# A two-layer decoder trunk with routed experts: the rows of expert 0 gathered apart from those of its group

## The chip, the core and the metric

The kernel runs on one core of a Trainium2 chip. The metric is device time in microseconds (us) of one execution, as the median of several runs. A core has a tensor engine (PE; its weight loads are listed as PEld), a vector engine (DVE), a scalar engine (ACT), GpSimd (POOL), a sync engine (SP) whose queue issues nearly all transfers here, and 16 DMA engines that bring data from DRAM into SBUF. Matmul results land in PSUM, in eight banks of 512 float32 per partition.

## The reference, cut to what matters

Two layers, each a token mixer (forgetting attention, then retention) and a mixture of 32 SwiGLU experts in 4 groups. 256 tokens of width 1024. A router picks one group per token and two experts in it.

```python
D_MODEL = 1024; SEQ = 256; DEPTH = 2
N_GROUPS = 4; EXPERTS_PER_GROUP = 8; N_EXPERTS = 32; TOP_K = 2; EXPERT_FF = 512

def hier_moe(h, wr_g, br_g, wr_e, br_e, w_gu, w_down):
    p_group = jax.nn.softmax((xf @ wr_g).astype(F32) + br_g.astype(F32), axis=-1)
    pg, gi = lax.top_k(p_group, 1)
    ...
    pv, pi = lax.top_k(jax.nn.softmax(e_in, axis=-1), TOP_K)
    gates = pg * pv / jnp.sum(pv, axis=-1, keepdims=True)
    expert_id = gi * EXPERTS_PER_GROUP + pi
    return grouped_experts(xf, expert_id, gates, w_gu, w_down).reshape(B, S, D)

# grouped_experts: for every expert e, on the rows xb of its tokens
    a, b = jnp.split(xb @ w_gu[e], 2, axis=-1)
    return (jax.nn.silu(a) * b) @ w_down[e]

def reference(...):
    h = x
    for i in range(DEPTH):
        hn = rms_norm(h, norm_mix[i])
        if i % N_MIXERS == 0:
            h = h + forgetting_attention(hn, fox_w_in[j], fox_b_f[j], fox_w_out[j])
        else:
            h = h + retention(hn, ret_w_in[j], ret_gn_gain[j], ret_w_out[j])
        hn = rms_norm(h, norm_ffn[i])
        h = h + hier_moe(hn, ...)
    return rms_norm(h, norm_final)
```

The expert weights are most of the bytes: a gate and up matrix of 4 MB and a down matrix of 2 MB for each of 32 experts in each of two layers.

## The kernel before

**Weights.** SBUF holds 26 slots of 1 MB. One list names every weight in the order of use (attention, experts of layer 0, retention, experts of layer 1). `Stream.pump` walks that list on SP's queue: it issues the next transfer as soon as enough slots are free, beyond a number held back (`st.reserve`). `st.done(key)` gives a slot back after the last matmul that reads it, and the transfer that takes the slot waits on SP for that matmul. Of experts 0 to 9 and of 31 (`pieces(e) == 2`) the gate and up matrix comes as four transfers of 1 MB and the down matrix as two; the others come in transfers of 2 MB. Order on every engine is the order of the program text (`manual_schedule`).

**The router.** `phase_moe` begins when the residual rows `h` of the layer are complete. DVE works out the mask `mkf` of chosen experts; three small matmuls with triangular and all-ones matrices count ranks; `rk` (line 950) then holds, per token and expert, the token's place among that expert's rows (0 if it is not chosen). Each expert has up to `CAP` = 32 rows.

**The gather of a group of four experts.** `one_hots(g4)` (lines 954 and 956) builds `oh`, for two halves of 128 tokens and four experts a matrix of 32 columns each: 1 where the place is right, times the token's `rstd` (the norm's factor). `gather(xg, tag, tag_T)` then takes the rows of all four experts at once, as 128 rows by 1024, in two steps: `rows(n)` multiplies `oh` with half of the width of `h` (line 967, a float32 matmul of 512 columns is two instructions) and ACT copies the result to SBUF (line 968); `turn(n)` transposes four chunks of 128 columns on PE (line 974), and DVE multiplies them by the norm's gain on the way out of PSUM (line 975). The result `xg` holds eight chunks `kk` of 128 by 128, with 32 columns for each of the four experts.

**An expert.** `first_product` computes the gate and up product in eight chunks `kk` (line 1044, 64 instructions), giving back a slot after every second chunk for experts in 1 MB pieces; ACT takes the silu (line 1053), DVE multiplies (line 1054) and transposes (line 1061). The second product (line 1072, 32 instructions) uses the down matrix. Eviction is split between DVE and ACT (lines 1087, 1085). After four experts `scatter` adds the group's results into PSUM sums.

**Around expert 0.** `start(part)`, called in the first product of expert 0, places the gate values' DVE chain (`gates`, lines 991 to 1008) behind chunk 1, sets `st.reserve = 1` behind chunk 5, and claims a slot for scratch behind chunk 7; another scratch slot is claimed behind the second product. So the first, second and third of the four slots that expert 0's first product gives back are filled with new weights at once, and the next transfer takes a slot of expert 0's down matrix. The gather of the next group stands behind the third expert of each group; only that of experts 0 to 3 stands ahead of the first product of its group.

Of the kernel before, what the change touches and what calls it, by code (L numbers as in the profile page):

```python
# [17 lines left out]
ALU = mybir.AluOpType  # L18
# [3 lines left out]
P = 128  # L22
# [6 lines left out]
CAP = 32  # L29
# [198 lines left out]
def trunk(ctx, tc, x, fox_w_in, fox_b_f, fox_w_out, ret_w_in, ret_gn_gain, ret_w_out,  # L228
# [3 lines left out]
    mm = nc.tensor.matmul  # L232
    V, A, G, PE = nc.vector, nc.scalar, nc.gpsimd, nc.tensor
# [5 lines left out]
    def bank(tag, dtype=F32):  # L239
        bufs = {"acc": 4, "sc": 2, "pt": 1, "o": 1}[tag]  # L240
        return ps.tile([P, 512], dtype, name=tag, tag=tag, bufs=bufs)
# [123 lines left out]
    iota = cst[:, C_IOTA:C_IOTA + CAP]  # L365
# [551 lines left out]
    def phase_moe(l, g, reserve_after, ahead, before_last, between):  # L917
# [31 lines left out]
        keep_warm(3)  # L949
        V.scalar_tensor_tensor(rk, b[:, 0:64].rearrange("p (t e) -> p t e", t=2), 1.0, mkf, ALU.add, ALU.mult)  # L950

        def one_hots(g4):

            V.tensor_tensor(oh, rk[:, :, 4 * g4:4 * g4 + 4, None].to_broadcast([P, 2, 4, CAP]),
                            iota[:, None, None, :].to_broadcast([P, 2, 4, CAP]), ALU.is_equal)
            V.tensor_tensor(oh, oh, rstd[:, :, None, None].to_broadcast([P, 2, 4, CAP]), ALU.mult)  # L956

        def gather(xg, tag, tag_T):

            o = oh.rearrange("p t e s -> p t (e s)")  # L960
            halves = [xg[:, 4 * n:4 * n + 4, :] for n in range(2)]
            flat = [v.rearrange("p c q -> p (c q)") for v in halves]

            def rows(n):
                b = bank(tag)
                for t in range(2):
                    mm(b, o[:, t, :], h[:, t, 512 * n:512 * n + 512], start=t == 0, stop=t == 1)  # L967
                A.activation(flat[n], b, AF.Copy)

            def turn(n):  # L970
                b = bank(tag_T)
                hv = flat[n].rearrange("p (q c) -> p c q", c=4)
                for c in range(4):
                    PE.transpose(b[:, P * c:P * c + P], hv[:, c, :], ident)  # L974
                V.tensor_tensor(halves[n], b.rearrange("p (c q) -> p c q", c=4),  # L975
                                gT[:, gi, 4 * n:4 * n + 4, None].to_broadcast([P, 4, P]), ALU.mult)

            rows(0)
            rows(1)
            turn(0)  # L980
            turn(1)

        one_hots(0)
        gather(g.xg, "acc", "acc")


        mm(b[:, 64:96], onb, mkf[:, 0, :], start=False, stop=False, skip_group_check=True)
# [46 lines left out]
        def first_product(e, e4, xg, after_part):  # L1034
            bgu = bank("sc")
            for part in range(4):
                n = 2 // pieces(e)
                key = "gu", l, e, part // n
                w = st.get(key)[:, 2 * (part % n):2 * (part % n) + 2, :]
                for k in range(2):  # L1040
                    kk = 2 * part + k
                    wv = w[:, k, :].rearrange("p (two f) -> p two f", two=2)
                    for j in range(4):
                        mm(bgu[32 * j:32 * j + 32, 0:256].rearrange("p (two f) -> p two f", two=2),  # L1044
                           xg[:, kk, 32 * e4:32 * e4 + 32], wv[:, :, P * j:P * j + P],
                           start=kk == 0, stop=kk == 7, skip_group_check=True)
                if part % n == n - 1:
                    st.done(key)
                if WARM <= e < NE - 1:
                    keep_warm(2, "pt")  # L1050
                after_part(part)
            sl, gg, gTt = w2["sl"], w2["gg"], w2["gT"]
            A.activation(sl, bgu[:, 0:P], AF.Silu)  # L1053
            V.tensor_tensor(gg.rearrange("p (c q) -> p q c", c=4), sl.rearrange("p (q c) -> p q c", c=4),  # L1054
                            bgu[:, P:2 * P].rearrange("p (q c) -> p q c", c=4), ALU.mult)
            return gg, gTt

        def turned(gg, gTt):


            V.transpose(gTt, gg)

        def expert(e, e4, xg, y4, after_part):
            gg, gTt = first_product(e, e4, xg, after_part)
            turned(gg, gTt)
            by = bank("o")
            n = 4 // pieces(e)
            for j in range(4):
                key = "wd", l, e, j // n
                w = st.get(key)  # L1070
                for nb in range(4):
                    mm(by[32 * nb:32 * nb + 32, 0:256], gTt[:, 32 * j:32 * j + 32],  # L1072
                       w[:, j % n, 256 * nb:256 * nb + 256], start=j == 0, stop=j == 3, skip_group_check=True)
                if j % n == n - 1:
                    st.done(key)
                if j == 1 and e >= WARM:
                    keep_warm(2, "sc")
            if e == 0:
                third()
                y4 = w2["y4"][0]  # L1080
            for nb in range(4):
                o = y4[32 * e4:32 * e4 + 32, 256 * nb:256 * nb + 256]
                i = by[32 * nb:32 * nb + 32, 0:256]
                if nb % 2:
                    A.activation(o, i, AF.Copy)  # L1085
                else:
                    V.tensor_copy(o, i)  # L1087
# [490 lines left out]
```

## Time and profile before

| | |
|---|---|
| Median of 3 runs | 1248.16 us (1246.19 to 1248.6) |
| Profiled execution | 1251.0 us, of which span 1248.9 us |
| PE busy | 982.5 us (79%) |
| DVE busy | 414.3 us (33%) |
| ACT busy | 317.6 us (25%) |
| DMA | 462.20 MB, 90.8% of 16 engines' span on SP's queue |
| Line 967 (rows of a group) | 72.8 us in 112 instructions to one kind of bank, and 16 more to another |
| Line 1044 (gate and up product) | 277.4 us in 4096 instructions |

The span is the time from the first to the last instruction of the profiled execution; the execution's own time is 2.1 us longer. Layer 0's router starts at about 163 us of the span and layer 1's at about 803 us. Busy shares are averages over stretches with different limits, so the stretches around the two routers have to be read by themselves. In a row of the timeline the first number is the start and the second the length of a run of equal instructions (xN says how many); in brackets stands the idle time before it and what ended it.

### The profile page before, as it was taken

What the parts mean: (1) busy time and instruction counts of PE and PEld (TensorE: products, weight loads), DVE (VectorE), ACT (ScalarE), POOL (GpSimd) and SP (SyncE); (2) the same over time, 40 slices, a digit from 0 to 9 for tenths busy, and PEclk for the clock granted to TensorE, in tenths of its full rate; (3) what the DMA queues carried; (4) which work ended last, traced back from release to release, by engine and by line L of the source; (5) the groups of instructions that cost most, each with busy time, mean ns of one, the idle gap of its engine ahead of it and who ended that gap; (6) DMA issues with size and microseconds to landing.
All of it is one profiled execution on the core that took longest, in us unless ns stands there. A gap on an engine that the chain in (4) does not pass through costs nothing.

```text
span 1248.9 us, 21544 instructions
## 1 busy us (share of the span) xinstructions
PE 982.5 (79%) x9223; PEld 634.3 (51%) x9223; DVE 414.3 (33%) x927; ACT 317.6 (25%) x672; POOL 42.8 (3%) x49
## 2 busy tenths in 40 slices
PE   8999986777575756678999999977776767677777
PEld 8888863343232323334889888744332323233333
DVE  5676832121111111111677676422121111111112
ACT  5665621111010100100554575321110111010112
POOL 2000000000000000000133100000000000000000
PEclk9999999899887879898999999989999888888979
DMA  9975879999999999999992768889999999999995
GB/s 339 321 264 192 321 279 421 419 427 426 427 426 427 428 428 426 427 426 394 378 335 69 268 237 308 332 357 419 423 427 428 427 427 427 427 427 427 428 424 192
DMA packets 74406, 462.20 MB, mean 370 GB/s; under 512 B 8881, under 2 KB 13761, under 8 KB 42050
## 3 DMA queue, kind: packets, MB, share of 16 engines
q1 hardware_dynamic: 73600, 460.17, 90.8%
q8 instruction: 74, 1.21, 0.4%
q10 hardware_dynamic: 706, 0.60, 0.2%
q14 instruction: 26, 0.21, 0.0%
HBM read 459.70 MB, written 1.05 MB: 369 GB/s over the span
## 4 chain that ended last, share of the span: by engine, by line
DMA 49%; PE 29%; DVE 2%; issue 1%; ACT 1%; POOLq 0%; ACTq 0%; SPq 0%; DVEq 0%
DMA slot<-in_expert_w_gu_dram 29%; DMA slot<-in_expert_w_down_dram 19%; PE sc L1044 5%; PE acc L495 4%; PE acc L509 3%; PE acc L507 3%; PE acc L508 3%; PE o L1072 3%; PE sc L967 1%; PE acc L1098 1%; DMA slot<-in_ret_w_in_dram 1%; DVE slot L1087 1%; PE pt L528 0%; PE acc L1138 0%; ACT slot L1085 0%
## 5 line engine op out<-in xcount | busy, mean ns | idle before, releaser
L1044 PE MATMUL sc<-slot,slot 128*32 128x256 f32 x4096 | 277.4, 422 | 54.9 <-DMA slot<-in_expert_w_gu_dram 51.8
L1044 PEld LDWEIGHTS sc<-slot,slot 128*32 128x32 f32 x4096 | 138.5, 119 | 181.4 <-issue 69.6
L1072 PE MATMUL o<-slot,slot 128*32 128x256 f32 x1984 | 137.8, 422 | 101.4 <-DMA slot<-in_expert_w_down_dram 58.7
L1072 PEld LDWEIGHTS o<-slot,slot 128*32 128x32 f32 x1984 | 70.8, 119 | 164.8 <-issue 80.2
L1054 DVE TENSOR_TENSOR slot<-slot,sc 128x128 f32<-128x128 f32 x64 | 23.7, 371 | 388.2 <-ACT slot L1053 388.2
L462 DVE SCALAR_TENSOR_TENSOR slot<-slot,gT,slot 128x512 fp32r<-128x512 f32 x160 | 123.9, 794 | 52.3 <-ACT slot L451 50.9
L495 PE MATMUL acc<-slot,slot 128*128 128x256 f32 x960 | 125.8, 288 | 1.6 <-ACT slot L451 1.1
L451 ACT ACTIVATE slot<-slot,gT 128x512 fp32r<-128x512 f32 x160 | 111.4, 718 | 38.6 <-PE acc L495 15.4
L495 PEld LDWEIGHTS acc<-slot,slot 128*128 128x128 f32 x960 | 118.9, 193 | 4.2 <-ACT slot L451 1.7
L1087 DVE COPY slot<-o 32x256 f32<-32x256 f32 x124 | 51.8, 418 | 204.3 <-PE o L1072 177.1
L1085 ACT ACTIVATE slot<-o 32x256 f32<-32x256 f32 x124 | 46.5, 375 | 281.5 <-DVE slot L1087 281.5
L1053 ACT ACTIVATE slot<-sc 128x128 f32<-128x128 f32 x64 | 17.7, 277 | 374.4 <-PE sc L1044 374.4
L507 PE MATMUL acc<-slot,slot 128*128 128x512 f32 x256 | 102.5, 400 | 0.0
L508 PE MATMUL acc<-slot,slot 128*128 128x512 f32 x256 | 100.0, 391 | 2.1 <-DVE slot L462 2.1
L509 PE MATMUL acc<-slot,slot 128*128 128x512 f32 x256 | 100.1, 391 | 0.0
L967 PE MATMUL sc<-h,slot 128*128 128x512 f32 x112 | 72.8, 811 | 33.5 <-DVE slot L956 33.5
L1098 PE MATMUL acc<-slot,slot 128*128 128x512 f32 (+1 forms) x128 | 60.9, 611 | 13.4 <-ACT slot L1085 13.2
L967 PEld LDWEIGHTS sc<-h,slot 128*128 128x128 f32 x112 | 27.7, 258 | 74.6 <-issue 74.6
L508 PEld LDWEIGHTS acc<-slot,slot 128*128 128x128 f32 x256 | 48.2, 188 | 11.8 <-DVE slot L462 2.8
L509 PEld LDWEIGHTS acc<-slot,slot 128*128 128x128 f32 x256 | 48.0, 188 | 10.2
L507 PEld LDWEIGHTS acc<-slot,slot 128*128 128x128 f32 x256 | 48.2, 188 | 9.3 <-issue 0.3
L975 DVE TENSOR_TENSOR slot<-pt,gT 128x512 f32<-128x512 f32 x28 | 19.4, 691 | 96.5 <-PE pt L974 96.5
(237 smaller groups left out, 750.6 us busy)
## 6 DMA issues: line engine op xcount, KB each, us to landing
slot<-in_expert_w_gu_dram SPq DMA_DIRECT2D x84, 2048.0 KB, 39.1
slot<-in_expert_w_gu_dram SPq DMA_DIRECT2D x86, 1024.0 KB, 13.4
slot<-in_expert_w_down_dram SPq DMA_DIRECT2D x42, 2048.0 KB, 39.1
slot<-in_expert_w_down_dram SPq DMA_DIRECT2D x40, 1024.0 KB, 13.3
slot<-in_ret_w_in_dram SPq DMA_DIRECT2D x24, 1024.0 KB, 14.1
slot<-in_fox_w_in_dram SPq DMA_DIRECT2D x15, 1024.0 KB, 11.8
slot<-in_ret_w_out_dram SPq DMA_DIRECT2D x8, 1024.0 KB, 7.3
slot<-in_fox_w_out_dram SPq DMA_DIRECT2D x4, 1024.0 KB, 14.6
```

The source lines that it names most:

```text
L451: A.activation(wh, w, AF.Copy, scale=1.0 if g is None else g)
L462: V.scalar_tensor_tensor(wl, w, g, wh, ALU.mult, ALU.subtract)
L495: mm(o, w[:, P * j:P * j + P], x[:, k, :], start=first and k == 0 and j % 2 == 0, stop=last and k == 7, skip_group_check=True)
L507: mm(banks[t], xh[:, q], wh, start=first and k == ks[0], stop=False)
L508: mm(banks[t], xh[:, q], wl, start=False, stop=False)
L509: mm(banks[t], xl[:, q], wh, start=False, stop=last and k == ks[-1])
L967: mm(b, o[:, t, :], h[:, t, 512 * n:512 * n + 512], start=t == 0, stop=t == 1)
L1044: mm(bgu[32 * j:32 * j + 32, 0:256].rearrange("p (two f) -> p two f", two=2), xg[:, kk, 32 * e4:32 * e4 + 32], wv[:, :, P * j:P * j + P], ...
L1072: mm(by[32 * nb:32 * nb + 32, 0:256], gTt[:, 32 * j:32 * j + 32], w[:, j % n, 256 * nb:256 * nb + 256], start=j == 0, stop=j == 3, skip_gr ...
L1085: A.activation(o, i, AF.Copy)
L1087: V.tensor_copy(o, i)
L1098: mm(sums[t, n], w2["scm"][0:rows, P * t:P * t + P], y4[0:rows, 512 * n:512 * n + 512], start=start, stop=False, skip_group_check=True)
```

## The change

Expert 0 of each layer no longer takes its columns from the group's `xg`. Two DVE instructions build its one-hot columns alone (rank compare and factor in one step); 16 matmuls, two halves of tokens for each of eight chunks, take 128 columns of `h` (every fourth one) as the stationary operand and the 32 one-hot columns as the moving one, so that the result `x0` comes out as chunks that need no transposing. All eight chunks lie in one PSUM bank; DVE evicts four at a time with the gain. `one_hots(0, 1)` then builds the columns of experts 1 to 3, and the gather of the whole group stands between the first and the second product of expert 0. `x0` lies in the first two of the eight chunks of `g.xg`, which that gather later overwrites. The same code runs in both layers.

```diff
--- before.py
+++ after.py
@@ -949,11 +949,13 @@
         keep_warm(3)
         V.scalar_tensor_tensor(rk, b[:, 0:64].rearrange("p (t e) -> p t e", t=2), 1.0, mkf, ALU.add, ALU.mult)
 
-        def one_hots(g4):
-
-            V.tensor_tensor(oh, rk[:, :, 4 * g4:4 * g4 + 4, None].to_broadcast([P, 2, 4, CAP]),
-                            iota[:, None, None, :].to_broadcast([P, 2, 4, CAP]), ALU.is_equal)
-            V.tensor_tensor(oh, oh, rstd[:, :, None, None].to_broadcast([P, 2, 4, CAP]), ALU.mult)
+        def one_hots(g4, i=0):
+
+            n = 4 - i
+            V.tensor_tensor(oh[:, :, i:4, :], rk[:, :, 4 * g4 + i:4 * g4 + 4, None].to_broadcast([P, 2, n, CAP]),
+                            iota[:, None, None, :].to_broadcast([P, 2, n, CAP]), ALU.is_equal)
+            V.tensor_tensor(oh[:, :, i:4, :], oh[:, :, i:4, :],
+                            rstd[:, :, None, None].to_broadcast([P, 2, n, CAP]), ALU.mult)
 
         def gather(xg, tag, tag_T):
 
@@ -980,8 +982,20 @@
             turn(0)
             turn(1)
 
-        one_hots(0)
-        gather(g.xg, "acc", "acc")
+
+        x0 = g.xg[:, 0:2, :].rearrange("p a (k s) -> p (a k) s", s=CAP)
+        for t in range(2):
+            V.tensor_scalar(oh[:, t, 0, :], iota, rk[:, t, 0:1], rstd[:, t:t + 1], ALU.is_equal, ALU.mult)
+        bx = bank("acc")[:, 0:8 * CAP].rearrange("p (k s) -> p k s", k=8)
+        for n in range(2):
+            for c in range(4):
+                for t in range(2):
+                    hv = h[:, t, 512 * n:512 * n + 512].rearrange("p (q c) -> p c q", c=4)
+                    mm(bx[:, 4 * n + c, :], hv[:, c, :], oh[:, t, 0, :], start=n == 0 and c == 0 and t == 0,
+                       stop=t == 1, skip_group_check=True)
+            V.tensor_tensor(x0[:, 4 * n:4 * n + 4, :], bx[:, 4 * n:4 * n + 4, :],
+                            gT[:, gi, 4 * n:4 * n + 4, None].to_broadcast([P, 4, CAP]), ALU.mult)
+        one_hots(0, 1)
 
 
         mm(b[:, 64:96], onb, mkf[:, 0, :], start=False, stop=False, skip_group_check=True)
@@ -1061,8 +1075,10 @@
             V.transpose(gTt, gg)
 
         def expert(e, e4, xg, y4, after_part):
-            gg, gTt = first_product(e, e4, xg, after_part)
+            gg, gTt = first_product(e, e4, xg if e else x0, after_part)
             turned(gg, gTt)
+            if e == 0:
+                gather(xg, "acc", "acc")
             by = bank("o")
             n = 4 // pieces(e)
             for j in range(4):
```

On PE, at the start of the experts of layer 0, before (the names: `acc`, `sc` and `o` are PSUM banks, `slot_124` the slot with the router's data, `oh` and `xg`; a bracket names the engines or transfers that the first instruction waits for):

```order
L528 MATMUL o<-ones 128x128 x2
L967 MATMUL acc<-h,slot_124 128x512 [waits DVE_49]
L967 MATMUL acc<-h,slot_124 128x512 x3
L974 MATMUL acc<-ident,slot_124 128x128 [waits Activation_49]
L974 MATMUL acc<-ident,slot_124 128x128 x3
L974 MATMUL acc<-ident,slot_124 128x128 [waits Activation_49]
L974 MATMUL acc<-ident,slot_124 128x128 x3
L987 LDWEIGHTS onb
L987 MATMUL sc<-mkf,onb 128x32
L988 LDWEIGHTS onb
L988 MATMUL sc<-mkf,onb 128x32
L1044 MATMUL sc<-slot_135,slot_124 32x256 [waits DMAHW5_49,DMAHW1_49,DVE_49]
```

and now:

```order
L528 MATMUL o<-ones 128x128 x2
L994 MATMUL acc<-slot_124,h 128x32 [waits DVE_49] x2
L994 MATMUL acc<-slot_124,h 128x32 x6
L994 MATMUL acc<-slot_124,h 128x32 [waits DVE_49]
L994 MATMUL acc<-slot_124,h 128x32 x7
L1001 LDWEIGHTS onb
L1001 MATMUL sc<-mkf,onb 128x32
L1002 LDWEIGHTS onb
L1002 MATMUL sc<-mkf,onb 128x32
L1058 MATMUL sc<-slot_135,slot_124 32x256 [waits DMAHW5_49,DMAHW1_49]
```

Four wide matmuls and eight transposes ahead of the first product became sixteen narrow matmuls, with a wait for DVE in their middle, at the ninth; the first product itself (line 1044, now 1058) has lost its own wait for DVE.

On PE, from the end of expert 0's first product to the first chunk of expert 1, before:

```order
L1044 MATMUL sc<-slot_989,slot_124 32x256 x7
L1072 MATMUL o<-slot_991,slot_989 32x256 [waits DMAHW5_49,DVE_49,PE_49]
L1072 MATMUL o<-slot_991,slot_989 32x256 x7
L1072 MATMUL o<-slot_141,slot_989 32x256 [waits DMAHW6_49,DMAHW0_49]
L1072 MATMUL o<-slot_141,slot_989 32x256 x7
L1044 MATMUL sc<-slot_143,slot_124 32x256 [waits DMAHW7_49]
```

and now:

```order
L1058 MATMUL sc<-slot_989,slot_124 32x256 x7
L969 MATMUL acc<-h,slot_124 128x512 [waits DVE_49]
L969 MATMUL acc<-h,slot_124 128x512 x3
L976 MATMUL acc<-ident,slot_124 128x128 [waits Activation_49]
L976 MATMUL acc<-ident,slot_124 128x128 x3
L976 MATMUL acc<-ident,slot_124 128x128 [waits Activation_49]
L976 MATMUL acc<-ident,slot_124 128x128 x3
L1088 MATMUL o<-slot_991,slot_989 32x256 [waits DMAHW5_49,DVE_49]
L1088 MATMUL o<-slot_991,slot_989 32x256 x7
L1088 MATMUL o<-slot_141,slot_989 32x256 [waits DMAHW6_49,DMAHW0_49]
L1088 MATMUL o<-slot_141,slot_989 32x256 x7
L1058 MATMUL sc<-slot_143,slot_124 32x256 [waits DMAHW7_49,DVE_49]
```

The group's gather (now lines 969 and 976) moved in whole to the place between the two products of expert 0. SP's queue issues the same transfers in the same order as before.

## Rows read from the trace of the kernel before

**Rows 1.** Page, part 4: the chain that ended last, by engine.
```profile
DMA 49%; PE 29%; DVE 2%; issue 1%; ACT 1%; POOLq 0%; ACTq 0%; SPq 0%; DVEq 0%
```
**Rows 2.** Stretches: PE, PEld, DVE, ACT, POOL busy, then PE clock, DMA share, GB/s.
```profile
170.00:175.00 5.00, 4.72 (x43) 2.78 (x46) 1.66 (x5) 2.72 (x4) 0.00 (x0) 1.00 0.00 0
...
810.00:815.00 5.00, 4.72 (x50) 2.88 (x52) 2.03 (x8) 3.17 (x5) 0.00 (x0) 1.00 0.02 3
...
740.00:750.00 10.00, 10.00 (x49) 8.17 (x48) 7.74 (x13) 7.06 (x12) 0.00 (x0) 1.00 0.46 156
...
280.00:560.00 280.00, 187.20 (x2030) 92.32 (x2029) 41.73 (x100) 27.40 (x72) 0.00 (x0) 0.87 1.01 427
860.00:1200.00 340.00, 235.88 (x2616) 116.50 (x2612) 53.89 (x130) 35.15 (x93) 0.00 (x0) 0.88 1.01 426
```
**Rows 3.** Timeline of PE and DVE around the first expert of layer 0.
```profile
167.24 0.23 DVE L950 SCALAR_TENSOR_TENSOR slot<-sc,mkf 128x64 f32<-128x64 f32 x1 [0.46 <-PE sc L948]
167.50 0.43 DVE L954 TENSOR_TENSOR slot<-slot,cst 128x256 f32<-128x256 f32 x1
167.96 0.42 DVE L956 TENSOR_TENSOR slot<-slot,rstd 128x256 f32<-128x256 f32 x1
168.44 3.70 PE L967 MATMUL acc<-h,slot 128*128 128x512 f32 x8 [0.60 <-DVE slot L956]
...
171.98 0.63 PE L974 MATMUL acc<-ident,slot 128*128 128x128 f32 x4
...
172.72 0.69 DVE L975 TENSOR_TENSOR slot<-acc,gT 128x512 f32<-128x512 f32 x1 [4.33 <-PE acc L974]
...
172.89 0.75 PE L974 MATMUL acc<-ident,slot 128*128 128x128 f32 x4 [0.28 <-ACT slot L968]
...
173.61 3.66 PE L1044 MATMUL sc<-slot,slot 128*32 128x256 f32 x64
...
178.47 1.93 PE L1072 MATMUL o<-slot,slot 128*32 128x256 f32 x32 [1.20 <-issue]
...
180.19 3.66 PE L1044 MATMUL sc<-slot,slot 128*32 128x256 f32 x64
```
**Rows 4.** Timeline: instructions of nearly the new ones' shapes.
```profile
162.18 1.96 PE L565 MATMUL pt<-wr,slot 128*128 128x36 f32 x16
...
164.73 0.39 DVE L932 SCALAR_TENSOR_TENSOR slot<-pt,rstd,rb 128x32 f32<-128x32 f32 x2
...
177.65 0.37 DVE L1054 TENSOR_TENSOR slot<-slot,sc 128x128 f32<-128x128 f32 x1 [0.50 <-ACT slot L1053]
```
**Rows 5.** SP's timeline in three short windows: issues at the restart of layer 0.
```profile
174.74 0.33 SPq L166 DMA_DIRECT2D slot<-in_expert_w_gu_dram  x1
...
176.47 0.69 SPq L166 DMA_DIRECT2D slot<-in_expert_w_gu_dram  x1
...
179.59 0.33 SPq L166 DMA_DIRECT2D slot<-in_expert_w_down_dram  x1
```
**Rows 6.** DMA issues, us to landing: those three, one at 800.48, one at 815.98.
```profile
slot<-in_expert_w_gu_dram SPq DMA_DIRECT2D x1, 1024.0 KB, 5.4
...
slot<-in_expert_w_gu_dram SPq DMA_DIRECT2D x1, 1024.0 KB, 8.9
...
slot<-in_expert_w_down_dram SPq DMA_DIRECT2D x1, 1024.0 KB, 8.3
...
slot<-in_expert_w_down_dram SPq DMA_DIRECT2D x1, 1024.0 KB, 5.6
...
slot<-in_expert_w_gu_dram SPq DMA_DIRECT2D x1, 1024.0 KB, 10.8
```
**Rows 7.** Page, part 6: the same kind over the whole span, median to landing.
```profile
slot<-in_expert_w_gu_dram SPq DMA_DIRECT2D x86, 1024.0 KB, 13.4
```
**Rows 8.** Layer 1, expert 2: timeline row, and the stretch around it.
```profile
828.76 5.35 PE L1044 MATMUL sc<-slot,slot 128*32 128x256 f32 x64
...
829.50:832.80 3.30, 3.30 (x36) 1.65 (x32) 0.00 (x0) 0.00 (x0) 0.00 (x0) 0.50 1.01 427
```

## The prediction

> **What bounds the kernel now.** I read the page's chain first: almost half of it is transfers, a third PE [rows 1]. The stretches then say where each holds. In the long middle of either layer's experts the 16 DMA engines are busy without a break (share 1.01 at 427 GB/s over 280 us, 426 over 340 us), while PE works two thirds of the time [rows 2]. There the end is set by the bytes, and only time in which the DMA engines stand still can be won. In the retention mixer between the two layers PE is busy 10.00 of 10 us [rows 2], so whatever layer 0 gains or loses arrives at layer 1's router undiminished.
>
> The DMA engines do stand still around each router: the stretch from 170 to 175 us moved 0 GB/s, that from 810 to 815 us moved 3 [rows 2]. All slots are full by then, and the next transfer has to wait until expert 0's first product gives back a slot. The SP rows show it: issue at 174.74 us, 1.13 us behind the start of that product at 173.61 [rows 3, 5]. So the path that counts is: ranks ready, gather, first two chunks of expert 0's product, issue. It occurs twice, once per layer, and layer 1's rows repeat layer 0's. A microsecond off it is a microsecond off the end, if the DMA engines, once started, don't run dry again.
>
> **The change part by part, for layer 0.** `rk` is ready at 167.24 + 0.23 = 167.47 us [rows 3].
>
> One-hots. Before, two DVE instructions on 256 columns end at 168.38, and PE starts 0.06 later [rows 3]. Now two on 32 columns. This kind with two pointer operands on 32 columns isn't in the rows; the nearest pair took 0.39 for both [rows 4], and I take that: the first ends at about 167.7, the second at 167.9. The bounds are half of it and the old 0.88. PE, which waits for the first alone and is just done with its keep-warm matmuls, starts at about 167.8.
>
> Sixteen float32 matmuls are 32 instructions, each with its own 128-column weight load. Sixteen of the same kind with 36 columns took 1.96 us [rows 4], 0.12 each; they load adjacent columns, here it is every fourth. Four transposes with such a load took 0.63 [rows 3], 0.16 each with the drain of the last one in it. So a half takes 1.96 to 2.5; I take 2.1, near the row of the same length. The first half ends at 169.9.
>
> Now the wait. The ninth matmul waits for DVE, and the order leaves only one candidate, the first eviction: the first product, which reads that eviction's result, no longer waits for DVE itself. The eviction starts some 0.1 later (172.61 to 172.72 before [rows 3]) and takes between 0.30 (an estimate: 0.69 for 512 columns less 384 at 1.02 ns, the slope between 0.43 for 256 and 0.69 [rows 3]) and 0.37 [rows 4]: I take 0.33, to 170.3, and PE goes on at 170.4. The second half ends at 172.5. The first product started 0.03 before the last transpose ended, with the same two rank matmuls between (172.89 + 0.75 = 173.64, against 173.61 [rows 3]). It now starts at 172.5 instead of 173.6: **1.1 us earlier**. The second eviction has 1.8 us (half of the product) to finish in and hides there, as do `one_hots(0, 1)` and the gates' chain on DVE, which only has to end before the gather on PE does. Bounds for this part: 0.7 (slow one-hots, slow eviction) to 1.7 (no wait).
>
> The wait falls under a rule. In the old gather each eviction had a bank of its own, so PE went from one half to the next with no wait for DVE (its two waits are for the one-hots and for ACT's copy [rows 3]), and the trace can't show the price. The Trainium skill, page "PSUM — Partial Sum Buffer", section "PSUM bank collisions raise a hardware error", says that a bank is to be guarded as a whole on a 32-partition quadrant, not by address, since matmul writes and vector reads there must not coincide. Two halves in one bank are thus serialised although they share no column. By that rule the gain is the 1.1 above, by addresses alone it would be 1.7.
>
> The gather that moves. Between the products PE so far idled 1.20 us waiting for silu, product and transpose [rows 3]. Now it runs the gather there: from 168.44 to the rank matmul at 173.48 it occupied 5.04 us of PE's order [rows 3]. It starts 3.5 us into the first product (3.66 less the 0.2 by which expert 1's product started ahead of the end of the second product: 178.47 + 1.93 against 180.19 [rows 3]), that is at 176.0, and the second product starts at 181.06, not 178.47: **2.6 us later**, expert 1 with it. Behind this wait stand, on PE, the second product and all of the experts; on SP, the transfers that take the slots they give back. ACT's two copies and DVE's two evictions for the gather come after silu and the transpose, and delay nothing.
>
> What is late next. The three issues of expert 0's first product come 1.1 earlier, at 173.65 to 175.4. The fourth takes a slot of expert 0's down matrix and follows the second product by 179.59 - 178.47 = 1.12 [rows 3, 5]: now at 182.2. The third landed at 176.47 + 8.9 = 185.4 [rows 5, 6], now at 184.3 if the data follow as before. The fourth, which found the engines busy, landed 2.5 later, at 179.59 + 8.3 = 187.9 [rows 5, 6]; now that would be 186.8. But it is issued only 2.1 us ahead of the third's landing, and a transfer issued to idle or nearly idle engines took 5.4 and 5.6 us [rows 6], which makes 187.6 to 187.8. So of the 1.1 us between 0.1 and 1.1 survive. I take **0.45** in layer 0, near the rows of 5.4, since the ramp of a fourth transfer overlaps the third's end. From the fifth on (expert 1's first at 182.8 + 1.13 = 183.9, then one per 0.87 us, half of 174.74 to 176.47 [rows 5]) the queue fills faster than one per 2.5 us drains it.
>
> Another price for a transfer from rest: the Trainium skill, page "DMA: Bandwidth & Descriptors", section "Anatomy of one DMA — SWDGE (gpsimd) path", gives about 2.0 us plus bytes at 436 GB/s for another path of issue, an estimated 4.4 us for 1 MB. The trace's 5.4 and 5.6 decide. With 4.4 the fourth would land at 186.6, never late, and the sum would be the full 2.2.
>
> In layer 1 the third transfer took 10.8 to land, not 8.9 [rows 6], so a late fourth has more time; I take 0.8 there, between the same bounds. PE's 2.6 us of lateness at expert 1 cost nothing later on: such a transfer takes 13.4 us from issue to landing over the span [rows 7], against some 5.5 from rest, so about 8 us of queue cover it.
>
> The sum: 0.45 + 0.8, about 1.2 us less. The profiled execution took 1251.0 us (span 1248.9 and 2.1 around it), so 1249.8 there. It lies 2.8 above the median of 1248.16; the terms are absolute, so the median becomes **1247.0 us**. A measurement of this kernel can tell about 0.2% from no change, 2.5 us: the forecast lies below that.
>
> **The rivals.** *No wait between the halves, and no dry queue.* Both layers gain 1.7: 3.3 less, 1244.9. For it: the columns are disjoint. Against: the order shows the wait. Chance 0.12.
>
> *The transfers run dry and restart from rest.* The fourth lands at 187.8 or later, where it landed before: nothing is won in either layer, 1248.2. For it: 5.6 us; against: the third is still in flight. Chance 0.17.
>
> *The clock falls between the two products: slower.* PE's granted clock is 1.00 (2.4 GHz) in the stretches around both routers; it was 0.50 (1.2 GHz) in the stretch from 829.5 us, early in layer 1's experts, and a first product took 5.35 us there instead of 3.66 [rows 2, 3, 8]. The new narrow matmuls and the stop between the halves are thin work for PE. If the clock falls there, first product or gather loses 1.7 us, the fourth transfer is issued at 183.9 and lands at 189.3, 1.4 later than before. It decides from an issue later than 182.5. In both layers that makes 2.8 more, 1251.0; against it stands that 36-column matmuls of the same step run just ahead of both routers and the clock held. Chance 0.08.
>
> *The gather of expert 0 is no shorter than the old one.* Had its instructions the 0.16 of the transposes [rows 3] in full, the 32 would take some 0.9 us more, and with an eviction of the old 0.69 the gain is gone. The product starts when it did, and the fourth transfer lands about 1.0 later: 1250.1. Chance 0.05.
>
> **How the numbers follow.** The forecast has the remaining 0.58, with 1246.0 to 1248.0 as its own range. Faster by over 0.2% (below 1245.7) takes the first rival, some of the forecast's edge and of the runs' own scatter of 2.4 us: 0.17. Slower by over 0.2% (above 1250.7) takes most of the clock rival and a little scatter: 0.08. The rest is 0.75. The range, 1244.8 to 1249.8, takes in the first rival, the dry queue and part of the slower ones.
>
> **What would show it.** Right: the first of the narrow matmuls some 0.6 us earlier than the old gather began; PE idle about 0.7 us on DVE at the ninth matmul; the first product 1.1 us earlier and the second 2.6 later behind `rk`; a fourth issue 8.5 us behind the first one instead of 4.9; a zero-traffic stretch shorter by 1.1 us, and a dip of the DMA share some 9 us behind the restart. Wrong: no idle time at the ninth matmul; a step other than 0.12; a second stretch of zero traffic of over 1 us; a granted clock below 1.00 between `rk` and expert 1; or PE waits for weights before about 280 us that were not there before.

## The result: slower, and the profile after

The changed kernel took 1260.24 us (median of 4, 1259.36 to 1261.41), the kernel before beside it 1247.78: ratio **1.0103** (95% interval 1.0088 to 1.0119), by that ratio some 12.8 us slower. The forecast was 1247.0, its range 1244.8 to 1249.8. Two executions in the experiments (2167 and 1340.8 us) ran slow throughout; the ratios leave them out, and no row here is from their profiles.

As before, the places to read are the two routers. PE in layer 0 and, from 809.90 on, in layer 1, to be held against [rows 3] (start, length, instruction, in brackets the idle time before it):

```profile
166.16 3.94 PE L994 MATMUL acc<-slot,h 128*128 128x32 f32 x16
170.48 3.94 PE L994 MATMUL acc<-slot,h 128*128 128x32 f32 x16 [0.38 <-DVE slot L996]
...
174.41 6.23 PE L1058 MATMUL sc<-slot,slot 128*32 128x256 f32 x64
180.57 3.70 PE L969 MATMUL acc<-h,slot 128*128 128x512 f32 x8
184.11 0.63 PE L976 MATMUL acc<-ident,slot 128*128 128x128 f32 x4
185.02 0.75 PE L976 MATMUL acc<-ident,slot 128*128 128x128 f32 x4 [0.28 <-ACT slot L970]
185.70 1.93 PE L1088 MATMUL o<-slot,slot 128*32 128x256 f32 x32
...
809.90 0.91 PE L528 MATMUL o<-ones 128*128 128x128 f32 x6
810.70 3.92 PE L994 MATMUL acc<-slot,h 128*128 128x32 f32 x16
815.00 3.94 PE L994 MATMUL acc<-slot,h 128*128 128x32 f32 x16 [0.38 <-DVE slot L996]
...
818.93 4.84 PE L1058 MATMUL sc<-slot,slot 128*32 128x256 f32 x64
```

The ranks (`rk`) are ready at 165.76 here (165.54 + 0.22, next fence) and were at 167.47 before, so all times are best counted behind them. A half of expert 0's gather takes 3.94 us instead of the 2.1 forecast, in both layers; the first product starts 8.65 us behind the ranks, before 6.14 [rows 3]; and it takes 6.23 us in layer 0 and 4.84 in layer 1 instead of 3.66. DVE, same stretch:

```profile
165.54 0.22 DVE L950 SCALAR_TENSOR_TENSOR slot<-sc,mkf 128x64 f32<-128x64 f32 x1 [0.46 <-PE sc L948]
165.80 0.51 DVE L988 TENSOR_SCALAR slot<-cst,slot,rstd 128x32 f32<-128x32 f32 x2
170.13 0.29 DVE L996 TENSOR_TENSOR slot<-acc,gT 128x128 f32<-128x128 f32 x1 [3.83 <-PE acc L994]
```

The stretches of after, to be held against [rows 2] (busy time of each engine, then PE clock, DMA share, GB/s):

```profile
166.20:169.40 3.20, 3.20 (x14) 3.20 (x15) 0.11 (x1) 0.00 (x0) 0.00 (x0) 1.00 0.02 8
169.50:179.60 10.10, 9.72 (x73) 6.79 (x76) 3.31 (x18) 1.55 (x2) 0.00 (x0) 0.50 0.22 65
...
814.60:821.30 6.70, 6.32 (x43) 5.08 (x46) 2.14 (x11) 1.03 (x2) 0.00 (x0) 0.50 0.00 0
186.00:188.00 2.00, 2.00 (x44) 1.23 (x40) 0.87 (x2) 0.00 (x0) 0.00 (x0) 1.00 0.32 74
```

The granted clock is 1.00 (2.4 GHz) in the first row and 0.50 (1.2 GHz) for some 10 us behind it, and so for 6.7 us in layer 1; the kernel before had no such stretch there. But the halves are as slow at 1.00 as at 0.50: in the 3.20 us of the first row 14 instructions fit, 0.23 each, and the second half, at 0.50, has the same 3.94. So two things went wrong, and only one is the clock. The weight loads show the first (count, then ns least, median, most):

```profile
L994 PEld LDWEIGHTS acc<-slot,h x64: 307/330/332, 166.2 to 818.5; 128*128 128x128 f32 x64
```

The kernel before loads the weights of [rows 4], adjacent columns in the same shape, in 192:

```profile
L565 PEld LDWEIGHTS pt<-wr,slot x64: 186/192/192, 157.3 to 803.5; 128*128 128x128 f32 x64
```

The last row of the stretches is the consequence: the DMA engines, restarted at 176.40, run short again at 186, since SP has nothing to issue (SP's rows, to be held against [rows 5]; xN issues from the start on):

```profile
176.40 3.74 SPq L166 DMA_DIRECT2D slot<-in_expert_w_gu_dram  x3
186.83 2.06 SPq L166 DMA_DIRECT2D slot<-in_expert_w_down_dram  x2
```

That fourth transfer then starts from rest, and its time from issue to landing is near the 5.4 of [rows 6]:

```profile
slot<-in_expert_w_down_dram SPq DMA_DIRECT2D x1, 1024.0 KB, 5.0
```

Behind the ranks the fourth issue comes at 21.06 us, before at 12.12. Counted from the packets that start behind the ranks, 16 MB have landed 6.7 us later than before in layer 0 and 4.1 later in layer 1 (4.8 if what is left of older transfers isn't counted): 10.8 to 11.5 of the 12.8. Later figures for 16 MB are counted in the first way, and in layer 1 they are as uncertain.

### The profile page after: what moved, and what is told of

Read it like the earlier page. It is cut to its first block, busy times and chain, and to the rows that moved or that the text cites. A ratio compares the mean times of both kernels' runs of the same rounds, so it can differ in the third digit from the quotient of the medians.

```text
span 1257.2 us, 21679 instructions
## 1 busy us (share of the span) xinstructions
PE 995.6 (79%) x9287; PEld 644.2 (51%) x9287; DVE 415.7 (33%) x935; ACT 317.4 (25%) x672; POOL 42.3 (3%) x49
## 5 line engine op out<-in xcount | busy, mean ns | idle before, releaser
L1058 PE MATMUL sc<-slot,slot 128*32 128x256 f32 x4096 | 283.3, 430 | 53.2 <-DMA slot<-in_expert_w_gu_dram 52.3
L969 PE MATMUL sc<-h,slot 128*128 128x512 f32 x112 | 69.1, 774 | 33.5 <-DVE slot L957 33.5
```

## The experiments

All compare with runs of the kernel before on the same chip. The theory at the start: the strided weight load and the fallen clock are two separate losses, and the moved gather of the group is not one. The rivals: the wait between the halves, or that gather, is the loss.

**Without expert 0's gather.** The 16 matmuls and two evictions are deleted; expert 0 works on stale rows.

```diff
-        bx = bank("acc")[:, 0:8 * CAP].rearrange("p (k s) -> p k s", k=8)
-        for n in range(2):
...
-                            gT[:, gi, 4 * n:4 * n + 4, None].to_broadcast([P, 4, CAP]), ALU.mult)
```

> The changed kernel with the 16 matmuls and two evictions for expert 0 left out (its first product reads what lies in x0, values of expert 0 wrong); the group's gather stays between the two products. It measures the move alone. Theory (the move is harmless as long as the gather ahead is short): first product about 1 us behind rk, first issue about 2, fourth issue about 10.5 us behind rk (before 12.1), 4 to 5 us less per layer, 1238 to 1241. Rival (the move itself costs: the transfers run dry while PE gathers, or the clock falls): 1246 or more.

Measured: 1239.31, ratio 0.9934 (0.9917 to 0.9950). The issues begin 1.5 us behind the ranks, the fourth comes at 10.2, and the clock does not fall within 20 us of the ranks. The group's gather between the products therefore costs nothing that the head start does not outweigh; the loss comes with the 16 matmuls and their evictions.

**Two banks.** Each half gets a PSUM bank, so the ninth matmul need not wait.

```diff
-        bx = bank("acc")[:, 0:8 * CAP].rearrange("p (k s) -> p k s", k=8)
         for n in range(2):
+            bx = bank("acc")[:, 0:4 * CAP].rearrange("p (k s) -> p k s", k=4)
...
```

> The changed kernel with the two halves of expert 0's chunks in two PSUM banks, so that no matmul waits for the first eviction. Theory (the wait is a small part): PE's idle time of 0.38 us at the ninth matmul goes, the first product starts 0.4 to 0.7 us earlier behind rk in each layer, time 1258.5 to 1260. Rival (the stop of PE between the halves is what lets the clock fall): granted clock 1.00 through the first product, time below 1255.

Measured: 1257.6, 1.0091 (1.0074 to 1.0108). PE of this kernel, layer 0:

```profile
165.81 7.68 PE L994 MATMUL acc<-slot,h 128*128 128x32 f32 x32
...
173.47 6.43 PE L1058 MATMUL sc<-slot,slot 128*32 128x256 f32 x64
```

The wait is gone, and with it 0.6 us up to the first product; the clock falls all the same, 3.5 and 4.0 us behind the ranks. The wait was real and small; the time is a little below the range of the theory and above that of the rival.

**Adjacent columns.** Each load takes 128 neighbouring columns instead of every fourth one (expert 0's rows come out in the wrong order).

```diff
-                    hv = h[:, t, 512 * n:512 * n + 512].rearrange("p (q c) -> p c q", c=4)
+                    hv = h[:, t, 512 * n:512 * n + 512].rearrange("p (c q) -> p c q", c=4)
```

> The changed kernel, but the 16 matmuls for expert 0 load 128 adjacent columns of h instead of every fourth (so the chunks hold other features and the values of expert 0 are wrong). Theory: the load of every fourth column for an ordinary float32 matmul takes 0.233 us whatever the clock, an adjacent one 0.11 to 0.12. Then a half takes 2.1 us instead of 3.94, the first product starts about 5.0 us behind rk (before 6.1, changed 8.65), the granted clock stays at 1.00 up to expert 1, and the time is 1246 to 1249. Rival 1, the loads are slow for another reason than the stride (32 moving columns, the shared bank): a half still takes 3.9 us, time about 1260. Rival 2, the fall of the clock comes with any narrow matmuls here: halves of 2.1 us, but clock 0.50 in the first product and 1250 to 1253.

Measured: 1252.33, 1.0046 (1.0030 to 1.0063). PE, layer 0:

```profile
165.97 1.97 PE L994 MATMUL acc<-slot,h 128*128 128x32 f32 x16
168.32 3.29 PE L994 MATMUL acc<-slot,h 128*128 128x32 f32 x16 [0.39 <-DVE slot L996]
...
171.60 5.58 PE L1058 MATMUL sc<-slot,slot 128*32 128x256 f32 x64
```
```profile
169.00:175.00 6.00, 6.00 (x47) 4.15 (x50) 2.74 (x16) 1.55 (x2) 0.00 (x0) 0.50 0.12 22
```

The first half has the length of [rows 4], 1.97 against 1.96: the stride alone had doubled it. But the clock falls 3.1 and 3.5 us behind the ranks, and takes second half and first product with it, as the second rival said. The stride is more than half of the loss, 7.1 of 12.8 us; the rest has another cause.

**Adjacent, every matmul twice.** If gaps in PE's work let the clock fall, twice the work should hold it.

```diff
+                    for i in range(2):
+                        mm(bx[:, 4 * n + c, :], hv[:, c, :], oh[:, t, 0, :],
...
```

> The adjacent loads, every matmul issued twice (values of expert 0 wrong): PE is occupied nearly as long as by the strided loads (64 instructions at 0.112 us, 7.2 us against 7.9) but with twice the matmuls. Theory (the duration makes PE late, and thin work makes the clock fall besides): clock 1.00 through the first product, first product about 8.3 us behind rk, fourth issue about 18, 1252 to 1256. Rival (the loss is the duration alone, the clock falls in any case or costs nothing): as the changed kernel, 1258 to 1261.

Measured: 1264.99, 1.0148 (1.0131 to 1.0165). The clock fell 4.2 and 3.1 us behind the ranks and stayed low for 10 and 14 us. In the stretch ahead of the first fall PE was busy throughout, 3.40 of 3.40 us:

```profile
166.50:169.90 3.40, 3.40 (x31) 3.40 (x32) 0.07 (x1) 0.00 (x0) 0.00 (x0) 1.00 0.06 24
170.00:179.50 9.50, 9.12 (x56) 8.04 (x59) 1.76 (x9) 0.58 (x2) 0.00 (x0) 0.51 0.01 2
```

The time lies above both ranges, and that gaps let the clock fall was not borne out; what was left to try was the width of the matmuls, 32 moving columns each.

**Adjacent and wide.** As above, with all four experts' 128 one-hot columns moving (only the first 32 results are used; expert 0's rows in the wrong order). Other than the expectation's words say, both halves use the same bank, one after the other, so the wait for the eviction stays; the next experiment does the same.

```diff
-                    mm(bx[:, 4 * n + c, :], hv[:, c, :], oh[:, t, 0, :], ...
+                    mm(bx[:, P * c:P * c + P], hv[:, c, :], oh[:, t].rearrange("p e s -> p (e s)"), ...
```

> The changed kernel with two edits: each weight load of expert 0's gather takes 128 adjacent columns instead of every fourth (so expert 0's values are not the reference's), and each of its matmuls has 128 moving columns (the one-hots of all four experts, of which only the first 32 results are taken up), each half with a bank of its own. The run with adjacent columns and 32 moving ones kept a first half of 1.97 us, but its clock fell to 0.50 at 3.1 and 3.5 us behind the ranks and its time was 1252.3. Theory (it is the narrow moving side that lets the clock fall): here the clock holds 1.00 until the first product has ended in both layers, the halves take some 2.0 to 2.5 us each, the first product starts 5 us behind the ranks and takes 3.7, the fourth issue comes at about 14.7, and the time is 1246 to 1249. Rival (the clock falls because of what PE did before, whatever the width): a stretch at 0.50 begins 3 to 4.5 us behind the ranks here too, and the time stays at 1252 or above.

Measured: 1248.39, 1.0021 (1.0011 to 1.0031). PE, layer 0:

```profile
165.93 2.05 PE L994 MATMUL acc<-slot,h 128*128 128x128 f32 x16
168.36 2.05 PE L994 MATMUL acc<-slot,h 128*128 128x128 f32 x16 [0.39 <-DVE slot L996]
...
170.39 3.66 PE L1058 MATMUL sc<-slot,slot 128*32 128x256 f32 x64
...
179.10 1.93 PE L1088 MATMUL o<-slot,slot 128*32 128x256 f32 x32
```

Four times the columns, the same length per half, and the clock holds at 1.00 until expert 2, 25 us behind the ranks, in both layers. The first product starts 4.85 us behind the ranks (forecast 5.0), the fourth issue comes at 14.70 (forecast 14.7). This is the forecast's own course, and still it isn't faster. Stretches of this kernel, first up to the end of the first product, then where the fourth and fifth transfers run:

```profile
166.00:174.00 8.00, 7.62 (x99) 5.76 (x99) 3.28 (x19) 1.55 (x2) 0.00 (x0) 1.00 0.19 55
...
177.00:179.00 2.00, 1.72 (x10) 1.19 (x8) 0.69 (x1) 0.60 (x1) 0.00 (x0) 1.00 1.02 426
179.00:181.00 2.00, 2.00 (x38) 1.20 (x40) 0.69 (x1) 0.00 (x0) 0.00 (x0) 1.00 0.84 356
181.00:183.00 2.00, 2.00 (x44) 1.17 (x36) 0.83 (x2) 0.75 (x2) 0.00 (x0) 1.00 0.91 246
183.00:185.00 2.00, 1.49 (x28) 0.65 (x20) 0.07 (x1) 0.28 (x1) 0.00 (x0) 1.00 1.08 365
185.00:187.00 2.00, 1.26 (x24) 0.97 (x28) 0.61 (x2) 0.00 (x0) 0.00 (x0) 1.00 0.92 348
```

At full flow it is 426 GB/s; for some 6 us behind the late fourth issue it is 246 to 365. The first MB lands 1.4 and 1.3 us earlier than before, the sixth 0.5 later and 0.2 earlier, and 16 MB 0.3 later and 0.3 earlier: the head start is given back.

**Strided and wide**, run twice: the changed kernel with the 128 moving columns alone.

```diff
-                    mm(bx[:, 4 * n + c, :], hv[:, c, :], oh[:, t, 0, :], ...
+                    mm(bx[:, P * c:P * c + P], hv[:, c, :], oh[:, t].rearrange("p e s -> p (e s)"), ...
```

> The changed kernel with 128 moving columns in each matmul of expert 0's gather (the one-hots of all four experts, of which only the first 32 results are taken up), each half with a bank of its own; weight loads take every fourth column as in the changed kernel. Theory (two separate causes: the strided weight load steps 0.233 us at any clock, and narrow matmuls let the clock fall): a half still takes 3.9 us, the clock holds, the first product starts some 8.3 us behind the ranks and takes 3.7 instead of 6.2 and 4.8, the fourth issue comes at about 18 instead of 21, and the time is 1251 to 1256. Rival (the strided load itself is the sparse work that lets the clock fall): the clock falls to 0.50 at 3.5 to 4.2 us behind the ranks as in the changed kernel, and the time is 1258 to 1260.

> The same kernel as the one with strided weight loads and 128 moving columns, once more, since its first profile shows an execution of 2167 us in which the whole core ran slow and can't be read; its four other times were 1255.2 to 1258.3, ratio 1.0083. Theory (two causes, with the late fourth transfer making both dearer than their own time): the clock holds 1.00 through the first product, the halves take 3.9 us each, the first product starts 8.3 to 8.6 us behind the ranks and takes 3.7, the fourth issue comes at 18.3 to 18.5, the first 16 MB have landed some 3.5 to 4.5 us later than before in either layer, and the time is 1255 to 1258. Rival (the strided load lets the clock fall too): a stretch at 0.50 before the first product has ended, and a first product of over 4.5 us.

Measured: 1257.14, 1.0083 (1.0068 to 1.0099), and 1255.35, 1.0065 (1.0051 to 1.0080). PE of the second, layer 0, and a stretch in layer 1:

```profile
166.01 4.00 PE L994 MATMUL acc<-slot,h 128*128 128x128 f32 x16
170.40 4.00 PE L994 MATMUL acc<-slot,h 128*128 128x128 f32 x16 [0.38 <-DVE slot L996]
...
174.37 3.66 PE L1058 MATMUL sc<-slot,slot 128*32 128x256 f32 x64
```
```profile
813.80:817.10 3.30, 3.30 (x16) 3.24 (x16) 0.00 (x0) 0.00 (x0) 0.00 (x0) 0.50 0.00 0
```

The halves stay at 4.0, the first product starts 8.75 and 8.84 us behind the ranks and is back at 3.66 in both layers, the fourth issue comes at 18.6. The first time is above the 1251 to 1256 expected, the second within its range. In layer 1 the clock did fall, for 3.4 us inside the second half, which took 4.10 there, and was back ahead of the first product; so for the strided form "wide holds the clock" is true of one layer in two, and the first half of the rival, that the strided load itself lets the clock fall, isn't excluded.

**A probe of the stride.** Within each half the four chunks are loaded with steps of 1, 2, 4 and 8 columns (expert 0's values are not the reference's).

```diff
+                    s = (1, 2, 4, 8)[c]
+                    hv = h[:, t, :].rearrange("p (q c) -> p c q", c=s)[:, :, 0:P]
...
```

> The changed kernel as a probe of the weight load: of the four chunks of each half, the first is loaded from adjacent columns, the second from every second, the third from every fourth, the fourth from every eighth (all from the row's start, so expert 0's values are not the reference's). Theory (the load's time is set by how far apart the columns lie in SBUF): 0.12 a step for adjacent columns, 0.23 for every fourth, every second between them or equal to one of them, every eighth 0.23 or more. Rival (any step other than one column costs the same): 0.12 and then 0.23 three times. Time some 1258, not to be compared closely.

Measured: one time, 1256.7. Weight loads of the first half, at clock 1.00, four to a chunk; each row begins with the last load of the chunk before:

```profile
166.39 0.66 PEld L995 LDWEIGHTS acc<-slot,h 128*128 128x128 f32 x5
...
166.86 1.13 PEld L995 LDWEIGHTS acc<-slot,h 128*128 128x128 f32 x5
...
167.66 1.04 PEld L995 LDWEIGHTS acc<-slot,h 128*128 128x128 f32 x4
```

From 166.39 to 166.86 are four steps of the chunk with every second column: 0.118, as in the adjacent chunk (0.11). From 166.86 to 167.66 are one such step and three with every fourth column: 0.23; the step of eight has 0.24. So a step of two float32 loads at nearly full speed, one of four at half, and one of eight hardly slower than that. The rival fell, since a step of two costs next to nothing. The Trainium skill, page "SBUF — State Buffer", section "Door 1: The DMA port swizzle", says that SBUF has lines of 16 bytes and that at least two hits in a line are needed for full bandwidth. By that a step of two float32 would be free and one of four would not, as here; the same passage also gives 4 fp32 as how far one can stride for free, and there the 0.23 decides. What the rule leaves open are the transposes of [rows 3], which load every fourth column too and step 0.12.

**Strips: narrow weights from adjacent columns.** Nothing is left out. The narrow one-hots become the weights (32 adjacent columns, four strips of PE) and `h`, every fourth column, the moving side with 256 columns; an ACT copy, two transposes and two evictions follow, with keep-warm matmuls between.

```diff
+            for j in range(4):
+                mm(bx[32 * j:32 * j + 32, 0:256].rearrange("p (n q) -> p n q", n=2), oh[:, t, 0, :], hv[:, j],
...
+        keep_warm(2)
+        A.activation(x0f, bx[:, 0:256], AF.Copy)
...
+            PE.transpose(bt[:, P * n:P * n + P], x0f[:, P * n:P * n + P], ident)
+        keep_warm(2)
```

> A candidate that computes everything: expert 0's rows are gathered the other way round, the 32-column one-hots as weights (eight narrow loads from adjacent columns, in four 32-column strips of PE) and h, every fourth column, 256 of them, as the moving side; one copy on ACT, two transposes, two evictions on DVE, and keep-warm matmuls behind the strips and behind the transposes. The group's gather stays between the two products as in the changed kernel. Theory (the strided weight load and the fall of the clock are the whole loss, and the idea of a short gather of expert 0 alone is sound): first product some 3 us behind the ranks at clock 1.00, first issue at 4.1, fourth at 12.7, 2 us less than before in each layer, 1242 to 1244; the run without any gather of expert 0, 1239.3, is its bound. Rival (a moving side that takes every fourth column is slow too, or the clock falls again): the strips take over 2 us or a stretch at 0.50 begins within 5 us behind the ranks, and the time is 1248 or above.

Measured: 1245.35, 0.9988 (0.9979 to 0.9997), above the 1242 to 1244 expected. The clock holds in both layers; the strips take 2.0 us, the first product starts 3.8 us behind the ranks (expected 3), the first issue comes at 4.94, 2.3 earlier than before. But the fourth comes at 13.65, 7 us behind the third, and 16 MB are ahead by only 0.7 and 1.4 us. PE, layer 0:

```profile
165.95 1.99 PE L994 MATMUL acc<-h,slot 128*32 128x256 f32 x16
...
169.37 3.66 PE L1065 MATMUL sc<-slot,slot 128*32 128x256 f32 x64
```

The two rows have the same shape and the same clock, but an instruction of the strips takes 0.124 us and one of the first product 0.057. The moving columns of the first product lie side by side, those of the strips are every fourth. So the stride, gone from the weights, seems to cost as much on the moving side: an estimated 1 us a layer (16 times the difference of these rows), about the 0.8 by which the first product comes later than expected. No run takes this stride away, so that cause is argued and not shown.

**Strips, the group's gather cut in two**, and **strips, all of it behind the second product.**

```diff
             if e == 0:
-                gather(xg, "acc", "acc")
+                rows, turn = gather(xg, "acc", "acc")
+                rows(0)
...
+            if e == 0:
+                rows(1)
+                turn(0)
+                turn(1)
```

This is the first of the two; in the second `rows(0)` stands behind the second product too.

> The kernel that gathers expert 0's rows in four strips, with the group's gather cut in two: the matmuls of its first half stay between expert 0's two products (1.85 us, about what PE stands idle there), those of its second half and the eight transposes go behind the second product. Nothing is left out. Theory (what the strips win is lost again because the fourth transfer is issued 7 us behind the third, and the DMA engines run short between): the first three issues stay at 4.9, 5.8 and 6.7 us behind the ranks, the fourth comes at 10.6 to 11.1 instead of 13.65, the fifth at some 15.5, and of the 1.9 us by which the first 6 MB land late against an unbroken stream about 1 comes back in each layer: 1243 to 1244. Rival (the loss against the strips' head start has another cause, and the order of the group's gather doesn't matter): the same 1245.4 within 0.6 us, or slower where expert 1's later fifth issue costs as much as the fourth gains.

> The same with the whole of the group's gather behind expert 0's second product, so that the second product follows the first as closely as before the change. Theory (dry queue): the fourth issue comes at 9.8 us behind the ranks, as near to the third as before; but expert 1's first issue, the fifth, moves to 16.7, some 1.5 us ahead of the landing of the fourth at 18.0, so that the shortage comes one transfer later: as much lost as with the gather between the products, 1244.5 to 1246. Rival (only the fourth transfer matters, later ones catch up): the full head start is kept, the first 6 MB land 2 us earlier than before, and the time is 1242 to 1243.

Measured: cut in two 1244.85, **0.9982** (0.9973 to 0.9991); all behind 1245.59, 0.9992 (0.9982 to 1.0003). PE and SP of the first, layer 0:

```profile
169.22 3.66 PE L1062 MATMUL sc<-slot,slot 128*32 128x256 f32 x64
172.81 1.98 PE L969 MATMUL acc<-h,slot 128*128 128x512 f32 x4
174.73 1.93 PE L1093 MATMUL o<-slot,slot 128*32 128x256 f32 x32
176.59 1.98 PE L969 MATMUL acc<-h,slot 128*128 128x512 f32 x4
```
```profile
170.35 2.06 SPq L166 DMA_DIRECT2D slot<-in_expert_w_gu_dram  x3
175.86 5.60 SPq L166 DMA_DIRECT2D slot<-in_expert_w_down_dram  x2
```

The fourth issue comes at 10.44 us, and the first 4 MB are 2.4 and some 3 us ahead of before; the fifth, now the late one, comes at 15.7, and 16 MB are ahead by some 1.5 and 2.3. Of the versions that compute everything this one has the lowest median, and its interval lies below 1. But 1244.85 is above the 1243 to 1244 expected and within 0.6 us of the uncut strips, as the rival said: that it beats them is what the transfers say, and the medians (0.5 us apart, intervals overlapping) don't show it, nor that it beats the third. The third lies in its range; how its transfers ran is not known.

## Why the prediction was wrong

- *One-hots*: right. PE starts 0.40 us behind the ranks, forecast 0.33.
- *"A half takes 1.96 to 2.5; I take 2.1"*: **the step that failed**. It took 3.94. The prediction saw that every fourth column is loaded, took its 2.1 from a row with adjacent columns [rows 4] and its upper bound of 2.5 from four transposes with such a load [rows 3]; for ordinary matmuls the same stride makes the step 0.23, whatever the clock, outside the bounds. Two halves make 3.7 us a layer. Its rival of a gather no shorter than the old one named this term, with 0.9 us and a chance of 0.05. Measured by taking the stride away, it cost 7.1 us over both layers with narrow matmuls (1.0103 to 1.0046) and 7.7 or 5.5 with wide ones (1.0083 or 1.0065 to 1.0021).
- *The wait at the ninth matmul*: right in kind, 0.38 us idle behind an eviction of 0.29 (forecast 0.33). For the idle time the prediction has two figures, 0.5 in its working (169.9 to 170.4) and 0.7 among its signs; both were too long. The halves share no column and still take turns; with a bank each they don't. That is the rule of the Trainium skill that the prediction cited (page "PSUM — Partial Sum Buffer", section "PSUM bank collisions raise a hardware error"), as the order enforces it; with a bank each the ratio was 1.0091 instead of 1.0103, within each other's intervals.
- *The clock*: the second failed step, given 0.08 as a rival. The argument against it, that 36-column matmuls run ahead of both routers at full clock [rows 4], rested on 16 instructions. All five kernels with 32 moving columns (after, two banks, adjacent, twice, probe) fell to 0.50 2.0 to 4.2 us behind the ranks, in both layers; the three with wide matmuls and an unstrided load (adjacent and wide, strips, strips cut in two) held it beyond 23 us in both. The price was put at 1.7 us in one product; it was 2.6 and 1.2 in the first product alone. Over the run, widening the matmuls gave back 2.5 or 4.7 us with the strided load (1.0103 to 1.0083 or 1.0065) and 3.1 with the adjacent one (1.0046 to 1.0021). What about narrow matmuls lets it fall is not settled. With stride and narrowness both gone, 10.2 of the 12.8 us are gone (1.0103 to 1.0021).
- *The gather between the products*: right. In the adjacent and wide kernel the second product starts 8.7 us behind the first, forecast 8.56, and without expert 0's gather the kernel is 8 us faster.
- *"From the fifth on the queue fills faster than it drains", net 0.45 and 0.8*: failed. With both losses removed the fourth transfer of layer 0 landed 19.84 us behind the ranks, 0.1 earlier than forecast (187.9 less 0.45 is 19.98 behind them); but the fifth landed 3.8 us after it, not 2.5, and the balance was nil in the transfers and 1.0021 in time. The rival of the dry queue, 1248.2, would have been nearest. Its 5.6 us [rows 6] is no row of a transfer from rest, as the engines moved 389 GB/s when it was issued; the fourth transfer of the changed kernel took 5.0. Why the time stands 1.4 to 3.9 us above the balance of its one profile is open in part: that profile is of an execution of 1247.44 us, 0.8 above the median before, while its median is 1248.39.

Two of the prediction's own signs of being wrong came true: a step other than 0.12, and a granted clock below 1.00 between `rk` and expert 1.

## What to carry to other kernels

Look at the column step of an operand, the stationary one above all, before pricing a matmul by a row with another step: the instruction's shape in the profile doesn't show it. A row that prices new work must match the work in step and width, and in how long it goes on; narrower matmuls in a row can cost the clock. And where three slots are freed early and the fourth late, count the transfers through to the first that finds the queue empty: a head start is worth only what that one leaves.

## What had not been expected of the hardware

- A float32 weight load of 128 columns, every fourth one: 0.330 us, a step of 0.233 at clock 1.00 and at 0.50; adjacent 0.19 and 0.112, every second column 0.118 a step, at 1.00. At 0.50 in the probe's second half the steps of the first two chunks were 0.213, so there the stride hardly costs anything.
- The granted clock fell to 0.50 behind a stretch in which PE was busy 3.40 of 3.40 us. The Trainium skill, page "TensorE: Matmul & The Clock Gate", section "HAM oscillation — how this bites in real kernels", tells of falls behind idle gaps of PE; these runs show one without.
- 128 moving columns cost hardly more than 32 beside a 128-column float32 weight load: 2.05 against 1.97 us for 16 instructions.
- Moving columns that are every fourth one went at less than half the speed of adjacent ones in rows of the same shape: 16 instructions of 256 in 1.99 us, against 64 in 3.66.
